# First loads of a fused QKV product: x by single row tiles between the k-tiles of the first weight block, each row tile cast and turned by itself

## The chip, the cores and the metric

The kernel runs on one core of a Trainium2 chip. A core has five engines with their own instruction streams: TensorE (PE in the profile, with its weight loads as PEld), VectorE (DVE), ScalarE (ACT), GpSimd (POOL) and SyncE (SP), which here only issues transfers. Sixteen DMA engines move data between HBM and the on-chip memory SBUF; PE writes its results into PSUM.

The metric is the device time of one execution in microseconds, lower is better. Runs of one kernel mostly agree within 0.2%. A change below 2% is classed as the same.

## The reference

```python
def setup_inputs():
    batch, seq, hidden = 16, 512, 768
    x = np.random.randn(batch, seq, hidden).astype(np.float32)
    w_qkv = np.random.randn(hidden, 3 * hidden).astype(np.float32)

def reference(x, w_qkv):
    qkv = np.matmul(x, w_qkv)          # 8192 x 768 times 768 x 2304
    q, k, v = ...                      # three column blocks of 768
    return np.stack([q, k, v], axis=0).astype(np.float32)
```

## The kernel before

x has 64 row tiles of 128 rows, handled in 32 pairs. w has four blocks of 512 columns and a remainder of 256 columns, each cut along the contraction into six k-tiles (KT = 6) of 128 rows. The first three pairs go through a plain bf16 product; from the fourth pair on, a form with seven products in place of eight is used, and by then all of w is on the chip. Only the start matters here.

Row tiles of x arrive in fp32 as rows and must be cast to bf16 and turned (transposed by PE through PSUM) before PE can use them; the k-tiles of w must be cast. While nothing has arrived, PE multiplies zeros (`busy`), to have its clock released.

```python
def load_rows(p):                      # a pair: two row tiles, one transfer of 786 kB
    xin[p] = xin_pool.tile([P, 2, K], fp32, name="xin")
    rows = x_flat[p * 2 * P:(p + 1) * 2 * P, :]
    nc.sync.dma_start(xin[p][:], rows.rearrange("(r m) k -> m r k", m=P))

def copy_halves(dst, src, two):        # half on DVE, half on ACT
    nc.vector.tensor_copy(out=dst[0], in_=src[0])
    if two:
        nc.scalar.activation(dst[1], src[1], ident)
    else:
        nc.vector.tensor_copy(out=dst[1], in_=src[1])

def turn_rows(p, two=True):            # cast_rows(p) is alike: fp32 -> bf16, by halves
    ...
    for r in range(2):
        cols = c[:, r, :].rearrange("m (p j) -> m j p", j=KT)
        ps = ps_pool.tile([P, KT, P], bf16, name="ps")
        for j in range(KT):
            nc.tensor.transpose(ps[:, j, :], cols[:, j, :], eye)
        ks = (slice(0, KH), slice(KH, KT))
        copy_halves([xb[p][:, n, r * P:(r + 1) * P] for n in ks], [ps[:, n, :] for n in ks], two)

# ---- order of the loads, all issued by SyncE
load_rows(0)
...
load_rows(1)
load_blocks(0, 0, 1)                   # six k-tiles of the first block, 262 kB each: k0..k5
load_w(st_rem[:], 0, KT, R_OFF, REM)   # the remainder, 786 kB
load_rows(2)
load_blocks(0, 1)                      # the next block in halves, and so on
...
# ---- order of the work
busy(11)
cast_rows(0)
turn_rows(0)
busy(4)
cast_rows(1)
cast_k(0)
cast_k(1)
turn_rows(1)
for j in range(2, KT):
    cast_k(j)
...                                    # remainder cast: half on ACT, half on DVE
block(0, 0, b1[0], singles, nothing)   # the first block, four row tiles, k-tile by k-tile
rem(0)
rem(1)
cast_rows(2, False)
turn_rows(2, False)
block(0, 0, b1[0], halves((4, 5)), nothing)
```

Of the kernel before, what the change touches and what calls it, by code (L numbers as in the profile page):

```python
# [10 lines left out]
def kernel(  # L11
# [20 lines left out]
    nc = tc.nc  # L32
    P = 128
# [3 lines left out]
    K = H  # L37
    N3 = w_qkv.shape[1]
    KT = K // P
    KH = KT // 2  # L40
    KC = K // 4
    NP = M // (2 * P)
    CB = 512
    REM = N3 - 4 * CB
    Q_OFF = (0, 2 * CB + REM)
    R_OFF = 2 * CB
    fp32 = mybir.dt.float32
    f32r = mybir.dt.float32r
    bf16 = mybir.dt.bfloat16
    ident = mybir.ActivationFunctionType.Identity  # L50
# [3 lines left out]
    x_flat = x.rearrange("b t h -> (b t) h")  # L54
# [5 lines left out]
    tq_pool = ctx.enter_context(tc.tile_pool(name="tq", bufs=2))  # L60
# [4 lines left out]
    xin_pool = ctx.enter_context(tc.tile_pool(name="xin", bufs=3))  # L65
    xf_pool = ctx.enter_context(tc.tile_pool(name="xf", bufs=2))
    xb_pool = ctx.enter_context(tc.tile_pool(name="xb", bufs=4))
    s_pool = ctx.enter_context(tc.tile_pool(name="s", bufs=2))
    ps_pool = ctx.enter_context(tc.tile_pool(name="ps", bufs=8, space=bass.MemoryType.PSUM))

    w_rem = w_pool.tile([P, KT, REM], bf16, name="w_rem")

    b1 = [w_pool.tile([P, KT, CB], bf16, name=f"b1_{q}") for q in range(2)]
# [7 lines left out]
    def load_w(dst, j0, nj, off, cols):  # L81
        rows = w_qkv.rearrange("(p j) n -> p j n", j=KT)
        nc.sync.dma_start(dst, rows[:, j0:j0 + nj, off:off + cols])

    stage = {}

    def load_blocks(q, c, nj=KH):
        if q == 0:
            t = tq_pool.tile([P, KT, CB], fp32, name="st0", tag="tq")
            for j in range(0, KT, nj):  # L90
                load_w(t[:, j:j + nj], j, nj, Q_OFF[q] + c * CB, CB)
            stage[q, 0, c], stage[q, 1, c] = t[:, :KH, :], t[:, KH:, :]
        else:
            for h in range(2):
                t = st_pool.tile([P, KH, CB], fp32, name="st1", tag="st")
                load_w(t[:], h * KH, KH, Q_OFF[q] + c * CB, CB)
                stage[q, h, c] = t[:]
# [11 lines left out]
    xin, xf, xb, sr = {}, {}, {}, {}  # L109
# [19 lines left out]



    def load_rows(p):
        xin[p] = xin_pool.tile([P, 2, K], fp32, name="xin")
        rows = x_flat[p * 2 * P:(p + 1) * 2 * P, :]
        nc.sync.dma_start(xin[p][:], rows.rearrange("(r m) k -> m r k", m=P))

    def copy_halves(dst, src, two):

# [5 lines that stand above are left out]

    xc = {}

    def cast_rows(p, two=True):
        src = xin.pop(p)
        xc[p] = s_pool.tile([P, 2, K], bf16, name="xc", tag="s")
        for r in range(2):  # L150
            halves = (slice(0, K // 2), slice(K // 2, K))
            copy_halves([xc[p][:, r, n] for n in halves], [src[:, r, n] for n in halves], two)

    def turn_rows(p, two=True):
        c = xc.pop(p)
        xb[p] = xb_pool.tile([P, KT, 2 * P], bf16, name="xb")
        for r in range(2):
            cols = c[:, r, :].rearrange("m (p j) -> m j p", j=KT)
            ps = ps_pool.tile([P, KT, P], bf16, name="ps")
            for j in range(KT):  # L160
                nc.tensor.transpose(ps[:, j, :], cols[:, j, :], eye)  # L161
            ks = (slice(0, KH), slice(KH, KT))
            copy_halves(
                [xb[p][:, n, r * P:(r + 1) * P] for n in ks], [ps[:, n, :] for n in ks], two
            )

    def round_x(p):
        xb[p] = xb_pool.tile([P, KT, 2 * P], bf16, name="xb")
# [42 lines left out]
    def bank():  # L211
        return ps_pool.tile([P, CB], fp32, name="ps")
# [29 lines left out]
    def rows_of(s, p, lo, hi):  # L242
        return out_flat[s, p * 2 * P:(p + 1) * 2 * P, lo:hi].rearrange("(r m) n -> m r n", m=P)

    def store_quad(u):
        if u.q == 0:
            nc.sync.dma_start(rows_of(0, u.p, 0, H), u.o[:, :, :H])
            nc.sync.dma_start(rows_of(1, u.p, 0, 2 * CB - H), u.o[:, :, H:])
        else:
            part = 2 * H - Q_OFF[1]  # L250
            nc.sync.dma_start(rows_of(1, u.p, H - part, H), u.o[:, :, :part])
            nc.sync.dma_start(rows_of(2, u.p, 0, H), u.o[:, :, part:])

    def rem_row(p, r, ps):
        for j in range(KT):
            nc.tensor.matmul(  # L256
                ps, xb[p][:, j, r * P:(r + 1) * P], w_rem[:, j, :],
                start=(j == 0), stop=(j == KT - 1), skip_group_check=True,
            )

    def rem(p):
        ps = ps_pool.tile([P, 2, REM], fp32, name="ps")
        for r in range(2):
            rem_row(p, r, ps[:, r, :])
        o = or_pool.tile([P, 2, REM], fp32, name="orem")
        nc.scalar.activation(o[:], ps[:], ident)  # L266
        nc.sync.dma_start(rows_of(1, p, R_OFF - H, R_OFF - H + REM), o[:])
# [70 lines left out]
    NS = 3  # L338
    zero = w_pool.tile([P, CB], bf16, name="zero")
    nc.vector.memset(zero[:], 0.0)  # L340
    load_rows(0)
    tiny = w_pool.tile([P, 1], fp32, name="tiny")
    nc.scalar.activation(tiny[:], zero[:, :1], ident)

    eye = w_pool.tile([P, 240], bf16, name="eye")[:, :P]
    make_identity(nc, eye)
    load_rows(1)
    load_blocks(0, 0, 1)
    st_rem = o_pool.tile([P, KT, REM], fp32, name="str", tag="o")
    load_w(st_rem[:], 0, KT, R_OFF, REM)  # L350
    load_rows(2)
    load_blocks(0, 1)
    load_blocks(1, 0)
    load_blocks(1, 1)
    load_x(3, nc.sync)
# [2 lines left out]
    def busy(n):  # L358

        ps = bank()  # L360
        for _ in range(n):
            nc.tensor.matmul(ps[:], zero[:, :P], zero[:], start=True, stop=True)  # L362
# [9 lines left out]
    def block(q, c, w, groups, cast_next):  # L372


        ps = {}
        for js, tiles in groups:
            for n in tiles:
                p, r = divmod(n, 2)
                if n not in ps:
                    ps[n] = bank()  # L380
                for j in js:
                    nc.tensor.matmul(  # L382
                        ps[n][:], xb[p][:, j, r * P:(r + 1) * P], w[:, j, :],
                        start=(j == 0), stop=(j == KT - 1), skip_group_check=True,
                    )
                if KT - 1 not in js:
                    continue
                if r == 0:
                    cast_next(p)
                u = quads[q][p]  # L390
                nc.scalar.activation(u.o[:, r, c * CB:(c + 1) * CB], ps[n][:], ident)
                if c == 1 and r == 1:
                    store_quad(u)

    def halves(tiles):
        return [(range(h * KH, (h + 1) * KH), tiles) for h in range(2)]


    singles = [((0, ), (0, 1)), ((1, ), (0, 1)), ((0, 1), (2, 3))]
    singles += [((j, ), range(4)) for j in range(2, KT)]  # L400

    act, dve = nc.scalar, nc.vector
    def cast_k(j):
        dve.tensor_copy(out=b1[0][:, j, :], in_=stage[0, j // KH, 0][:, j % KH, :])

    def cast_next(q, c, w):
        return lambda p: p < 2 and cast(q, p, c, w, act)

# [1 line left out]
        dve.tensor_copy(out=b1[0][:, j, :], in_=stage[0, j // KH, 0][:, j % KH, :])  # L410

    nothing = lambda p: None
    busy(11)
    cast_rows(0)
    turn_rows(0)
    busy(4)
    cast_rows(1)
    cast_k(0)
    cast_k(1)
    turn_rows(1)  # L420
    for j in range(2, KT):
        cast_k(j)
    act.activation(w_rem[:, KH:], st_rem[:, KH:], ident)
    dve.tensor_copy(out=w_rem[:, :KH], in_=st_rem[:, :KH])
    bt0 = bt_pool.tile([P, KT, CB], bf16, name="bt")
    bt1 = bt_pool.tile([P, KT, CB], bf16, name="bt")

    block(0, 0, b1[0], singles, nothing)
    rem(0)
    rem(1)  # L430
    cast_rows(2, False)
    turn_rows(2, False)
    block(0, 0, b1[0], halves((4, 5)), nothing)
    for h in range(2):
        cast(0, h, 1, bt0, dve)
    for n in range(1, 5):
        sum_w(0, n)
    dve.tensor_copy(out=b22[0][:], in_=stage[0, 1, 1])
    block(0, 1, bt0, halves(range(6)), cast_next(1, 0, b1[1]))
    load_x(4, nc.sync)  # L440
    block(1, 0, b1[1], halves(range(6)), cast_next(1, 1, bt1))
# [56 lines left out]
```

## Time and profile before

| | |
|---|---|
| time, median of 3 runs (later of 6) | 363.31 us (363.34) |
| span of the profiled execution | 362.0 us, itself a run of 363.8 us |
| PE busy | 353.5 us, 98% of the span |
| first real block matmul | 9.25 us |
| first remainder matmul | 14.43 us |
| first matmul of the next block | 20.61 us |
| last k-tile of the first block (k5) landed | 11.04 us |

The last four are the milestones to watch: all work of PE behind 20.61 us follows without a hole of note, so the end stands or falls with them.

### The profile page before, as it was taken

How to read it: one execution, taken by the hardware profiler on the slowest of the kernel's cores; microseconds unless marked ns; L12 is line 12 of the kernel's file. 1: busy time of each engine (PE TensorE's matmuls, PEld its weight loads, DVE VectorE, ACT ScalarE, POOL GpSimd, SP SyncE). 2: the span in 40 equal slices, each digit the busy share in tenths (PEclk: the TensorE clock that was granted, in tenths of full speed). 3: DMA queues.
4: the chain of work that ended last, by engine and by line, in shares of the span. 5: the costliest groups of instructions: out<-in, count | busy, mean ns of one | idle time of the engine just before them, and what ended most of it. 6: DMA issues, size and time to landing. Idle time of an engine off the chain costs nothing.

```text
span 362.0 us, 5220 instructions
## 1 busy us (share of the span) xinstructions
PE 353.5 (98%) x1765; PEld 248.6 (69%) x1797; DVE 224.4 (62%) x239; ACT 182.5 (50%) x304; POOL 174.1 (48%) x180
## 2 busy tenths in 40 slices
PE   8999999999999999999999999999999999999995
PEld 3644577777777776777777777777777777777763
DVE  3489746865566765566675565676556676556642
ACT  4547554445454545454545544444545454545452
POOL 0000960756664445664445665444666444666410
PEclk9999999999999999999999999999999999999999
DMA  7999969999999989899899999899989998989766
GB/s 295 381 381 339 346 224 343 331 304 298 278 321 298 295 275 295 282 313 313 284 277 294 281 306 316 281 283 285 295 284 317 295 295 274 300 275 332 266 251 242
DMA packets 80617, 108.08 MB, mean 299 GB/s; under 512 B 4816, under 2 KB 60368, under 8 KB 80592
## 3 DMA queue, kind: packets, MB, share of 16 engines
q1 hardware_dynamic: 65184, 96.35, 82.5%
q10 hardware_dynamic: 15408, 11.41, 9.7%
q8 instruction: 14, 0.23, 0.3%
q14 instruction: 11, 0.09, 0.1%
HBM read 32.24 MB, written 75.50 MB: 298 GB/s over the span
## 4 chain that ended last, share of the span: by engine, by line
PE 96%; ACT 1%; issue 1%; ACTq 0%; DVE 0%
PE ps L206 75%; PE ps L256 11%; PE ps L382 9%; PE ps L362 1%; PE ps L161 1%; ACT o L237 0%; ACTq L297 0%; ACT xb L141 0%; ACT orem L311 0%; DVE xb L139 0%; ACT xc L141 0%; ACTq L313 0%; DVE zero L340 0%; ACTq L311 0%
## 5 line engine op out<-in xcount | busy, mean ns | idle before, releaser
L206 PE MATMUL ps<-t,s 128*128 128x512 f32 x696 | 171.4, 395 | 0.0
L206 PEld LDWEIGHTS ps<-t,s 128*128 128x128 f32 x696 | 128.5, 188 | 26.5
L169 POOL CAST xb<-xf 128x1536 bf16<-128x1536 f32 x29 | 43.9, 1514 | 168.5 <-DVE xf L124 159.1
L234 DVE TENSOR_TENSOR o<-o,ps 128x512 f32<-128x512 f32 x58 | 39.9, 689 | 91.8 <-ACT o L233 91.8
L124 DVE STREAM_TRANSPOSE xf<-xin 128x1536 f32<-128x1536 f32 x29 | 85.5, 2950 | 5.7 <-DMA xin<-in_x_dram 2.9
L206 PE MATMUL ps<-b,xb 128*128 128x512 bf16 x320 | 74.2, 379 | 1.9
L206 PEld LDWEIGHTS <-xb 128*128 128x128 bf16 x348 | 31.7, 98 | 41.6 <-issue 7.3
L233 ACT ACTIVATE o<-ps 128x512 f32<-128x512 f32 x58 | 34.7, 598 | 44.7 <-PE ps L206 44.7
L240 DVE TENSOR_TENSOR o<-o,ps 128x512 f32<-128x512 f32 x58 | 39.9, 688 | 21.4 <-PE ps L206 20.2
L206 PE MATMUL ps<-b,s 128*128 128x512 f32 x174 | 48.7, 389 | 0.0
L256 PE MATMUL ps<-w_rem,xb 128*128 128x256 bf16 x384 | 47.2, 273 | 0.0
L266 ACT ACTIVATE orem<-ps 128x512 f32<-128x512 f32 x31 | 18.6, 601 | 56.3 <-PE ps L256 54.3
L237 ACT ACTIVATE o<-ps 128x512 f32<-128x512 f32 x58 | 34.7, 598 | 24.2 <-PE ps L206 21.4
L220 ACT ACTIVATE o<-ps 128x512 f32<-128x512 f32 x58 | 34.6, 597 | 23.8 <-DVE o L240 20.7
L256 PEld LDWEIGHTS <-xb 128*128 128x128 bf16 x384 | 37.4, 98 | 11.2 <-issue 0.5
L227 ACT ACTIVATE o<-ps 128x512 f32<-128x512 f32 x58 | 34.7, 599 | 6.6 <-PE ps L206 1.5
L224 DVE TENSOR_TENSOR o<-o,ps 128x512 f32<-128x512 f32 x58 | 36.4, 668 | 2.0 <-ACT o L220 1.3
L206 PEld LDWEIGHTS ps<-b,s 128*128 128x128 f32 x174 | 32.6, 188 | 6.9
L178 POOL TENSOR_TENSOR s<-s,xf 128x384 fp32r<-128x384 f32 x29 | 30.1, 1039 | 2.3
L177 POOL TENSOR_TENSOR s<-xf 128x384 fp32r<-128x384 f32 x29 | 31.0, 1069 | 0.0
L179 POOL TENSOR_TENSOR s<-xf 128x384 fp32r<-128x384 f32 x29 | 29.5, 1017 | 0.0
L181 POOL TENSOR_TENSOR s<-xf,s 128x384 fp32r<-128x384 f32 x29 | 29.5, 1016 | 0.0
(36 smaller groups left out, 129.3 us busy)
## 6 DMA issues: line engine op xcount, KB each, us to landing
out_dram<-o SPq DMA_DIRECT2D x62, 768.0 KB, 5.3
out_dram<-o SPq DMA_DIRECT2D x65, 256.0 KB, 4.5
xin<-in_x_dram SPq DMA_DIRECT2D x62, 192.0 KB, 6.7
xin<-in_x_dram ACTq DMA_DIRECT2D x54, 192.0 KB, 4.5
out_dram<-orem SPq DMA_DIRECT2D x31, 256.0 KB, 5.1
st<-in_w_qkv_dram SPq DMA_DIRECT2D x6, 768.0 KB, 14.1
xin<-in_x_dram SPq DMA_DIRECT2D x3, 768.0 KB, 5.7
st<-in_w_qkv_dram SPq DMA_DIRECT2D x6, 256.0 KB, 6.2
```

The source lines that it names most:

```text
L124: nc.vector.transpose(t[:].rearrange("p j (g b) -> p g j b", b=G), xin.pop(p)[:].rearrange("p g (a j) -> p g j a", a=G),)
L169: nc.gpsimd.tensor_copy(out=xb[p][:], in_=xf[p][:])
L206: nc.tensor.matmul(ps[:], lhs[j], rhs[j], start=(start and j == 0), stop=(j == KH - 1), skip_group_check=True,)
L220: nc.scalar.activation(c11, u.x[:], ident)
L224: nc.vector.tensor_tensor(c11, c11, u.z[:], op=add)
L227: nc.scalar.activation(c12, u.x[:], ident)
L233: nc.scalar.activation(c22, u.x[:], ident)
L234: nc.vector.tensor_tensor(c22, c22, u.y[:], op=add)
L237: nc.scalar.activation(c21, u.x[:], ident)
L240: nc.vector.tensor_tensor(c12, c12, u.y[:], op=add)
L256: nc.tensor.matmul(ps, xb[p][:, j, r * P:(r + 1) * P], w_rem[:, j, :], start=(j == 0), stop=(j == KT - 1), skip_group_check=True,)
L382: nc.tensor.matmul(ps[n][:], xb[p][:, j, r * P:(r + 1) * P], w[:, j, :], start=(j == 0), stop=(j == KT - 1), skip_group_check=True,)
```

## The change

The intent: give PE real work earlier. The first pairs of x come in row tiles of 393 kB, interleaved with the k-tiles, and every row tile is cast and turned as soon as it is there; PE then begins with two rows on two k-tiles while the rest is under way. The remainder and the third pair are cut in the same manner.

```diff
-    load_rows(0)
+    load_row(0, 0)                    # one row tile, [128, 768] fp32, 393 kB
 ...
-    load_rows(1)
-    load_blocks(0, 0, 1)
+    load_row(0, 1)
+    load_k(0)
+    load_k(1)
+    load_row(1, 0)
+    load_k(2)
+    load_row(1, 1)
+    for j in range(3, KT):
+        load_k(j)
-    load_w(st_rem[:], 0, KT, R_OFF, REM)
-    load_rows(2)
+    for h in range(2):
+        load_w(st_rem[:, h * KH:(h + 1) * KH], h * KH, KH, R_OFF, REM)
+    for r in range(2):
+        load_row(2, r)
 ...
-    busy(11)
-    cast_rows(0)
-    turn_rows(0)
-    busy(4)
-    cast_rows(1)
+    busy(8)
+    cast_row(0, 0)
+    cast_row(0, 1)
+    turn_row(0, 0)
+    busy(1)
     cast_k(0)
+    turn_row(0, 1)
     cast_k(1)
-    turn_rows(1)
 ...
+    def third_row():                  # busy(2), cast_row(1, 0), cast_k(2), turn_row(1, 0)
+    def fourth_row():                 # cast_row(1, 1), cast_k(3), turn_row(1, 1), cast_k(4), cast_k(5),
+                                      # then the remainder's cast, both halves on DVE
-    block(0, 0, b1[0], singles, nothing)
-    rem(0)
-    rem(1)
-    cast_rows(2, False)
-    turn_rows(2, False)
-    block(0, 0, b1[0], halves((4, 5)), nothing)
+    block(0, 0, b1[0], [
+        ((0, ), (0, 1)), ((1, ), (0, 1)), third_row,
+        ((2, ), (0, 1)), (range(3), (2, )), fourth_row,
+        ((3, ), range(3)), (range(4), (3, )), ((4, ), range(4)), ((5, ), range(4)),
+    ], nothing)
+    for p in range(2):
+        rem(p)
+        cast_row(2, p, False)
+        turn_row(2, p, False)
+    block(0, 0, b1[0], [(range(KT), (4, )), (range(KT), (5, ))], nothing)
```

More of the change, by code (lines that the diff above doesn't have):

```diff
@@ L128, in transpose, with load_row @@
         xf[p] = t
-    def load_rows(p):
-        xin[p] = xin_pool.tile([P, 2, K], fp32, name="xin")
-        rows = x_flat[p * 2 * P:(p + 1) * 2 * P, :]
-        nc.sync.dma_start(xin[p][:], rows.rearrange("(r m) k -> m r k", m=P))
+    def load_row(p, r):
+        if r == 0:
+            xin[p] = xin_pool.tile([P, 2, K], fp32, name="xin")
+        row = (2 * p + r) * P
+        nc.sync.dma_start(xin[p][:, r, :], x_flat[row:row + P, :])
     def copy_halves(dst, src, two):
@@ L145, with cast_row, turn_row @@
     xc = {}
-    def cast_rows(p, two=True):
-        src = xin.pop(p)
-        xc[p] = s_pool.tile([P, 2, K], bf16, name="xc", tag="s")
-        for r in range(2):
-            halves = (slice(0, K // 2), slice(K // 2, K))
-            copy_halves([xc[p][:, r, n] for n in halves], [src[:, r, n] for n in halves], two)
-    def turn_rows(p, two=True):
-        c = xc.pop(p)
-        xb[p] = xb_pool.tile([P, KT, 2 * P], bf16, name="xb")
-        for r in range(2):
-            cols = c[:, r, :].rearrange("m (p j) -> m j p", j=KT)
-            ps = ps_pool.tile([P, KT, P], bf16, name="ps")
-            for j in range(KT):
-                nc.tensor.transpose(ps[:, j, :], cols[:, j, :], eye)
-            ks = (slice(0, KH), slice(KH, KT))
-            copy_halves(
-                [xb[p][:, n, r * P:(r + 1) * P] for n in ks], [ps[:, n, :] for n in ks], two
-            )
+    def cast_row(p, r, two=True):
+        if r == 0:
+            xc[p] = s_pool.tile([P, 2, K], bf16, name="xc", tag="s")
+        halves = (slice(0, K // 2), slice(K // 2, K))
+        copy_halves([xc[p][:, r, n] for n in halves], [xin[p][:, r, n] for n in halves], two)
+    def turn_row(p, r, two=True):
+        if r == 0:
+            xb[p] = xb_pool.tile([P, KT, 2 * P], bf16, name="xb")
+        cols = xc[p][:, r, :].rearrange("m (p j) -> m j p", j=KT)
+        ps = ps_pool.tile([P, KT, P], bf16, name="ps")
+        for j in range(KT):
+            nc.tensor.transpose(ps[:, j, :], cols[:, j, :], eye)
+        ks = (slice(0, KH), slice(KH, KT))
+        copy_halves(
+            [xb[p][:, n, r * P:(r + 1) * P] for n in ks], [ps[:, n, :] for n in ks], two
+        )
     def round_x(p):
@@ L346, with load_k @@
     make_identity(nc, eye)
-    load_rows(1)
-    load_blocks(0, 0, 1)
-    st_rem = o_pool.tile([P, KT, REM], fp32, name="str", tag="o")
-    load_w(st_rem[:], 0, KT, R_OFF, REM)
-    load_rows(2)
-    load_blocks(0, 1)
+    st_0 = tq_pool.tile([P, KT, CB], fp32, name="st0", tag="tq")
+    stage[0, 0, 0], stage[0, 1, 0] = st_0[:, :KH, :], st_0[:, KH:, :]
+    def load_k(j):
+        load_w(st_0[:, j:j + 1], j, 1, Q_OFF[0], CB)
+    load_row(0, 1)
[6 more added lines that the diff above has]
+        load_k(j)
+    st_rem = o_pool.tile([P, KT, REM], fp32, name="str", tag="o")
+    for h in range(2):
+        load_w(st_rem[:, h * KH:(h + 1) * KH], h * KH, KH, R_OFF, REM)
+    for r in range(2):
+        load_row(2, r)
+    load_blocks(0, 1, KH)
     load_blocks(1, 0)
@@ L375, in block @@
         ps = {}
-        for js, tiles in groups:
+        for group in groups:
+            if callable(group):
+                group()
+                continue
+            js, tiles = group
             for n in tiles:
@@ L396, in halves @@
         return [(range(h * KH, (h + 1) * KH), tiles) for h in range(2)]
-    singles = [((0, ), (0, 1)), ((1, ), (0, 1)), ((0, 1), (2, 3))]
-    singles += [((j, ), range(4)) for j in range(2, KT)]
     act, dve = nc.scalar, nc.vector
-    def cast_k(j):
-        dve.tensor_copy(out=b1[0][:, j, :], in_=stage[0, j // KH, 0][:, j % KH, :])
     def cast_next(q, c, w):
@@ L412 @@
     nothing = lambda p: None
-    busy(11)
-    cast_rows(0)
-    turn_rows(0)
-    busy(4)
-    cast_rows(1)
+    busy(8)
[3 more added lines that the diff above has]
+    busy(1)
     cast_k(0)
+    turn_row(0, 1)
     cast_k(1)
-    turn_rows(1)
-    for j in range(2, KT):
-        cast_k(j)
-    act.activation(w_rem[:, KH:], st_rem[:, KH:], ident)
-    dve.tensor_copy(out=w_rem[:, :KH], in_=st_rem[:, :KH])
+    def third_row():
+        busy(2)
+        cast_row(1, 0)
+        cast_k(2)
+        turn_row(1, 0)
+    def fourth_row():
+        cast_row(1, 1)
+        cast_k(3)
+        turn_row(1, 1)
+        cast_k(4)
+        cast_k(5)
+        for h in range(2):
+            ks = slice(h * KH, (h + 1) * KH)
+            dve.tensor_copy(out=w_rem[:, ks], in_=st_rem[:, ks])
     bt0 = bt_pool.tile([P, KT, CB], bf16, name="bt")
     bt1 = bt_pool.tile([P, KT, CB], bf16, name="bt")
-    block(0, 0, b1[0], singles, nothing)
-    rem(0)
-    rem(1)
-    cast_rows(2, False)
-    turn_rows(2, False)
-    block(0, 0, b1[0], halves((4, 5)), nothing)
+    block(0, 0, b1[0], [
[8 more added lines that the diff above has]
+    block(0, 0, b1[0], [(range(KT), (4, )), (range(KT), (5, ))], nothing)
     for h in range(2):
```

## The prediction

> **What bounds the kernel now.** I read the page first (busy shares, then the chain that ended last), then the chain in order of time for the first 60 us, then the timelines of PE, DVE and ACT over the first 40 us, because the change touches nothing after them. From the page:
>
> ```profile
> PE 353.5 (98%) x1765; PEld 248.6 (69%) x1797; DVE 224.4 (62%) x239; ACT 182.5 (50%) x304; POOL 174.1 (48%) x180
> PE 96%; ACT 1%; issue 1%; ACTq 0%; DVE 0%
> ```
>
> PE is busy 98% of a span of 362.0 us and carries 96% of the chain. Whatever starts the real matmuls earlier moves the end by as much, as long as PE does not have to wait again later; nothing else can pay. So the prize is what PE does before it has real work. The chain in order of time (start us, us, what):
>
> ```profile
> 1.19 4.87 PE ps L362 x11
> 6.06 0.65 PE ps L161 x6
> ...
> 8.00 0.42 ACT xc L141
> 8.42 0.05 issue
> 8.47 0.95 PE ps L161 x12
> 9.42 2.16 PE ps L382 x10
> 11.57 0.05 issue
> 11.63 2.97 PE ps L382 x13
> 14.60 2.62 PE ps L256 x24
> 17.22 0.35 PE ps L161 x6
> 17.57 0.02 issue
> 17.59 0.37 DVE xb L139
> 17.96 0.05 issue
> 18.00 0.39 PE ps L382
> ```
>
> L362 is a matmul on zeros that keeps PE busy, L161 the transposes of x by PE, L382 the block matmuls, L256 the remainder columns. PE starts on real blocks at 9.25 us and then never rests for long: the one later hole is the turn of the third pair (17.57 to 18.00, 0.43 us). Before 9.25, real work is 24 transposes of 0.08 to 0.1 us, some 2.1 us; about 7 us of the first 9.25 are dummies or waiting. 7 us is 1.9% of 363.3, so even a perfect start would not reach 2%.
>
> What holds the start? The timeline of DVE (start us, us, instruction, the idle time before it and what ended it):
>
> ```profile
> 5.02 0.63 DVE L139 CAST xc<-xin 128x384 bf16<-128x384 f32 x2 [3.89 <-DMA xin<-in_x_dram]
> ...
> 11.06 0.43 DVE L410 CAST b<-st 128x512 bf16<-128x512 f32 x1 [0.24 <-DMA st<-in_w_qkv_dram]
> 13.30 0.56 DVE L424 CAST w_rem<-str 128x768 bf16<-128x768 f32 x1 [1.81 <-DMA str<-in_w_qkv_dram]
> 15.39 0.36 DVE L139 CAST xc<-xin 128x384 bf16<-128x384 f32 x1 [1.53 <-DMA xin<-in_x_dram]
> ...
> 20.95 0.96 DVE L370 CAST bt<-st 128x1536 bf16<-128x1536 f32 x1 [1.34 <-DMA st<-in_w_qkv_dram]
> ```
>
> DVE finds an empty input five times: the loads run at the pace of the DMA engines, and PE, with its work at 9.25, follows them closely. The trace's record of each landing gives: first pair of x rows 5.00 us, second 6.96, the six k-tiles of w 7.65, 8.31, 9.00, 9.68, 10.35, 11.04, the remainder columns 13.28, the third pair 15.27, the halves of the next block 17.30 and 20.92. A k-tile of 262 kB takes 0.68 us (385 GB/s), a pair of 786 kB 1.96 us (401 GB/s).
>
> **What the Trainium skill says.** "DMA: Bandwidth & Descriptors", Specifications, gives a fabric ceiling of 435 GB/s and an HBM limit of about 358 per core. The trace has 385 to 416 GB/s here, above the second and below the first; the measurement decides: the queue is already full, and smaller transfers will not make bytes arrive faster, only in another order. "TensorE: Matmul & The Clock Gate", Part 1, says that a matmul of 512 columns takes 426.7 ns on the idle clock and 215.7 on the full one, and that about 3.4 us of activity in a free-running window releases it. The trace agrees: the dummies are 0.43 us apart up to 5 us, 49 block matmuls take 10.74 us (219 ns each), and the clock record turns full at 6.64 us. Part 4 of that page says that transposes do not count as busy in the same way; no run shows this yet, and I use it as a risk.
>
> **The change part by part.** 4 of 15 dummies go (8, 1 and 2 remain). Each pair of rows comes in two transfers of 393 kB, between the k-tiles; the remainder in two as well. Row tiles are cast, turned and used singly, and PE's order is mixed: rows 0 and 1 on k-tiles 0 and 1, then row 2's turn, and so on. The remainder's cast goes from ACT and DVE to DVE alone in two halves. The third pair's turns are put one after each remainder product. Matmuls, transposes and bytes stay as they are. 4 transfers are added, which at 0.43 to 0.65 us of issue each stay ahead of 0.68 to 0.98 us of movement. The trace shows every ninth transfer being issued only when the first of the last eight landed (the ninth at 5.02, after 5.00; the tenth at 6.98, after 6.96); with smaller pieces, eight in flight are still above 2 MB, so the queue does not run dry.
>
> Landings, as estimates from those rates: row 0 at 4.0, row 1 at 5.0, k0 5.67, k1 6.34, row 2 7.3, k2 8.0, row 3 9.0, k3 9.66, k4 10.34, k5 11.0, remainder halves 12.15 and 13.28, rows 4 and 5 at 14.3 and 15.27. The last byte of each stage comes no sooner than before: k5 is where it was.
>
> PE then, with DVE casts and evictions of 0.35 to 0.37 us, ACT's of 0.49 to 0.52 (ACT's half of an eviction begins only where DVE's half ended: 7.13 after 6.74+0.37), k-tile casts of 0.42: 8 dummies end at 1.19+8x0.427=4.6, row 0 is turned by 5.3 and row 1 by 6.3. k0's cast ends at 6.2, row 1's eviction at 6.8, k1's cast at 7.2, so the first four block matmuls run from 6.3 to 7.7 with holes. Two dummies and row 2's turn take PE to 8.5, five matmuls to 9.6. Row 3 lands at 9.0, but ACT evicts row 2 first (9.0 to 9.47), so its cast ends at 9.99 and PE idles 0.4 us. Turn to 10.45, then 15 matmuls of 0.216 us = 3.24: 13.7 us against 14.43 before. The remainder's halves are cast by 12.7 and 13.84, in time to within 0.1.
>
> From there: 12 remainder matmuls 1.31, row 4's turn 0.42, 12 more 1.31 (16.75), row 5's turn after its cast (16.75 to 17.2), 12 block matmuls 2.59: the next block begins at 19.8 against 20.61. **Sum: 0.8 us**: 0.7 from the block that ends earlier (14.43-13.7), and 0.1 from the stretch after it, 6.18 us before (14.43 to 20.61, with its hole) and 6.1 now. All the rest of PE's work moves up by that, if the later inputs are there: the second half of the next block is cast by 21.9 and needed at 19.8+18x0.216=23.7; the block after lands at 22.79 and 24.82, needed at 27.5 and 31.4. In the first strided pair, PE needs the sums for its third product at about 48 and POOL has them by 43.0. In the later stage POOL is ahead by over 2 us. So the shift should reach the end whole.
>
> **Rivals.** (1) The clock is released later. PE is active from 1.19 in both, but in 3.1 to 6.5 us the new kernel has more transposes and only some 2 us of dummies. If the transposes don't count, the full clock comes 3.4 us later; about nine matmuls and two dummies at double time cost 2.3 us of which the waits for k-tiles absorb much, and the block ends near 14.4: gain 0.1 to 0.2. For: the skill; against: PE has hardly a gap there. One in four. (2) The loads bound all of it: k5, the remainder and row 5 land where they were, and the change yields nothing. Against: in the kernel before, PE begins the remainder 3.4 us after k5 lands, so there is something to win there. But the remainder's second half, landed at 13.28 and cast by 13.84, lets the second group of its matmuls go no earlier than that, which caps the gain near 0.9, and row 5 at 15.27 caps it near 1.5. (3) The extra turns between DVE and ACT cost more than is won: each of four row turns is a round of cast, transposes and two evictions in series, 0.35+0.65+0.37+0.49 us. If each waited 0.3 us more than I reckon, the block would end at 14.6 and the change would be neutral or 0.3 us slower. (4) Gain lost later: DMA engines are busy over 90% in the whole span, so loads of later x pairs might not move up and PE would give it back. The slack of over 2 us speaks against.
>
> **Range and chances.** Central step sum 363.3-0.8=362.5; weighting the later clock and the slower hand-overs, I take 362.6. The three runs before differ by 0.22 us; gains from -0.1 to 1.3 us give 362.0 to 363.4. 2% is 7.3 us, more than all the idle time at the start, so faster by that is out of reach; slower by that would need a stall of a kind that nothing here shows.
>
> **What would show it right or wrong.** First row cast at 4.0 us; first block matmul near 6.3; k5's cast at about 11.4 to 11.8; first remainder matmul at 13.7; first matmul of the next block at 19.8; the same landings from the remainder on. Full clock at 6.6 us in both kernels; if the dummies or matmuls near 8 us are 0.43 us apart, rival 1 holds. If the first remainder matmul waits for its cast, rival 2; if PE's waits at the row turns sum to over 1.5 us between 6.3 and 13.7, rival 3; if 19.8 is met but the end is not moved, rival 4. I am wrong in kind if the time moves by over 1.5 us either way.

## The result, and the profile after

The changed kernel took 363.81 us (median of 6 runs, 363.52 to 364.00) against 363.34 us for the kernel before in the same rounds (363.23 to 363.90). The ratio is 1.001 with a 95% interval of 0.9997 to 1.0023. A ratio is computed as the mean time of one kernel's runs over that of the other's of the same rounds, so it is not quite the ratio of the medians. The change is worth nothing, and leans to the slow side; I had predicted 362.6 us with 362.0 to 363.4 as the range.

The page of the changed kernel, the lines of busy time and of the chain by engine:

```profile
PE 352.8 (98%) x1761; PEld 247.4 (68%) x1793; DVE 225.6 (62%) x240; ACT 182.2 (50%) x303; POOL 173.8 (48%) x180
PE 95%; DMA 1%; ACT 1%; issue 1%; ACTq 0%; SPq 0%; DVE 0%
```

A new entry stands in the chain, DMA with 1%. The chain in order of time (start us, us, what) shows where it is:

```profile
2.12 4.96 DMA st<-in_w_qkv_dram
7.08 0.02 issue
7.10 0.44 DVE b L422
...
7.58 0.59 PE ps L401 x2
...
14.33 1.40 PE ps L255 x12
15.72 0.53 PE ps L160 x6
16.25 1.31 PE ps L255 x12
17.56 0.48 PE ps L160 x6
```

Before, the chain ran through PE's dummies and turns from 1.19 us on. Now it runs through one transfer of w, issued at 2.12 us and landed at 7.08: k1. The timeline of DVE shows the same from the side of the one who waits:

```profile
3.71 0.36 DVE L140 CAST xc<-xin 128x384 bf16<-128x384 f32 x1 [2.58 <-DMA xin<-in_x_dram]
...
5.62 0.43 DVE L422 CAST b<-st 128x512 bf16<-128x512 f32 x1 [0.15 <-DMA st<-in_w_qkv_dram]
...
7.10 0.43 DVE L422 CAST b<-st 128x512 bf16<-128x512 f32 x1 [0.75 <-DMA st<-in_w_qkv_dram]
...
13.95 0.56 DVE L448 CAST w_rem<-str 128x768 bf16<-128x768 f32 x1 [0.56 <-DMA str<-in_w_qkv_dram]
15.03 0.36 DVE L140 CAST xc<-xin 128x384 bf16<-128x384 f32 x1 [0.52 <-DMA xin<-in_x_dram]
```

k0 is cast at 5.62, as early as I had reckoned. k1 comes 1.48 us after it, where a k-tile took 0.68 us before. That transfer is the only one on the chain: from the end of k1's cast at 7.53 to the next block the chain is work alone, and the second trace of this kernel (e0_after) has the same shape, with k1 landing at 7.44. Everything behind is late by about that difference: k5 landed at 11.70 us instead of 11.04, the remainder's second half is cast from 13.95 instead of 13.30, the first remainder matmul starts at 14.16 instead of the 13.7 that I expected, and the next block at 20.47 instead of 19.8.

The rate of the loads over the first 10 us, in 40 slices of a quarter of a microsecond, first of the kernel before, then of the changed one:

```profile
GB/s 0 0 0 0 0 0 0 147 74 61 283 319 418 393 430 418 418 406 430 418 418 406 418 414 402 389 418 402 402 401 385 393 377 393 393 385 385 385 385 381
DMA packets 1340, 3.04 MB, mean 304 GB/s; under 512 B 113, under 2 KB 114, under 8 KB 1340
```

```profile
GB/s 0 0 0 0 0 0 0 233 184 246 307 418 381 356 418 381 340 340 344 271 205 184 254 254 369 369 414 389 332 389 279 381 397 414 422 356 385 393 385 418
DMA packets 1243, 2.80 MB, mean 280 GB/s; under 512 B 131, under 2 KB 131, under 8 KB 1243
```

Before, the rate stays at or above 377 GB/s from 3 us on. After, it falls to between 184 and 344 from 4 to 6 us. In ten microseconds 0.24 MB less arrive. The trace's record of single packets tells part of how: a packet of 2 kB normally takes 84 ns and one of 3 kB 121 ns. Between 3 and 8 us the changed kernel has 20 packets above 250 ns, the longest 1028 ns; the kernel before has none, its longest being 124 ns. I call them slow packets below. The count leaves out what comes before 3 us, where every kernel has some: 3 to 16 of them begin between 2 and 3 us, 7 in the kernel before and 9 in the changed one.

The count marks a disturbed start, but does not measure the loss. An estimate from these records: the 20 packets took 9.0 us together, where 15 of 2 kB and 5 of 3 kB would take 1.9 at their usual times; over 16 engines the difference is 0.44 us, of the 0.66 by which k5 was late. In the second trace of the changed kernel it is 0.34 of 1.0 us, in e6 below 0.15 of 0.9. From 3 to 7 us the time of all packets also fell from 102.8% to 95.2% of the sixteen engines' time, so engines stood without a packet more often than before.

### The profile page after: what moved, and what is told of

Its sections match the earlier page's. It is cut to its first block, busy times and chain, and to the rows that moved or that the text cites. A ratio compares the mean times of both kernels' runs of the same rounds, so it can differ in the third digit from the quotient of the medians.

```text
span 361.7 us, 5215 instructions
## 1 busy us (share of the span) xinstructions
PE 352.8 (98%) x1761; PEld 247.4 (68%) x1793; DVE 225.6 (62%) x240; ACT 182.2 (50%) x303; POOL 173.8 (48%) x180
## 4 chain that ended last, share of the span: by engine, by line
PE 95%; DMA 1%; ACT 1%; issue 1%; ACTq 0%; SPq 0%; DVE 0%
PE ps L205 75%; PE ps L255 11%; PE ps L401 8%; DMA st<-in_w_qkv_dram 1%; PE ps L160 1%; ACT o L236 0%; ACTq L296 0%; SPq L136 0%; ACT orem L310 0%; ACT xb L142 0%; DVE b L422 0%; PE ps L376 0%; SPq L83 0%; ACT xc L142 0%; ACTq L312 0%
```

## The experiments

My theory after the result is D: the interleaved order of the first loads makes them slower, and all of the lost gain is in that. Its rivals are E, that not the order but the cut into smaller transfers does it; H, that the new hand-overs between DVE, ACT and PE cost more than I reckoned; and C, that the moment of the clock's release is behind it. First all measurements in one table (e2 and t5 each had one run, of 367.1 and 366.7, that stands apart; the medians are hardly moved by it): times as medians against the kernel before of the same rounds, and from the trace of each run the landing of k5, the count of packets above 250 ns between 3 and 8 us, the start of the first block matmul and of the next block's, all in us.

| run | time | before | ratio (95%) | k5 landed | slow packets | first block | next block |
|---|---|---|---|---|---|---|---|
| before (first trace) | 363.34 | | | 11.04 | 0 | 9.25 | 20.61 |
| after (first trace) | 363.81 | 363.34 | 1.0010 (0.9997-1.0023) | 11.70 | 20 | 6.10 | 20.47 |
| e0_before | 363.59 | 363.28 | 1.0005 (0.9993-1.0017) | 10.99 | 0 | 9.21 | 20.56 |
| e0_after | 363.73 | 363.28 | 1.0009 (0.9997-1.0021) | 12.03 | 21 | 7.16 | 20.81 |
| e1_rows_first | 367.41 | 363.28 | 1.0109 (1.0096-1.0122) | 12.62 | 23 | 9.72 | 24.00 |
| e2_old_compute_new_loads | 364.90 | 363.28 | 1.0053 (1.0033-1.0072) | 11.67 | 23 | 10.55 | 21.91 |
| e3_pairs_between | 364.38 | 363.36 | 1.0027 (1.0014-1.0039) | 11.69 | 19 | 7.34 | 21.34 |
| e4_first_pair_whole | 364.50 | 363.36 | 1.0030 (1.0018-1.0043) | 11.70 | 18 | 7.30 | 21.58 |
| e5_cut_only | 364.56 | 363.36 | 1.0027 (1.0013-1.0041) | 12.51 | 22 | 9.65 | 21.53 |
| e6_cut_by_columns | 364.05 | 363.36 | 1.0021 (1.0008-1.0033) | 11.95 | 6 | 9.21 | 21.01 |
| g1_third_pair_only | 363.38 | 363.29 | 0.9997 (0.9985-1.0009) | 11.01 | 2 | 9.27 | 20.48 |
| v1_split_banks | 362.97 | 363.29 | 0.9988 (0.9975-1.0001) | 11.02 | 1 | 8.35 | 19.84 |
| t5_order_only | 364.91 | 363.29 | 1.0050 (1.0034-1.0065) | 11.48 | 15 | 10.19 | 21.54 |
| u1_new_compute_old_loads | 365.53 | 363.29 | 1.0058 (1.0046-1.0070) | 11.03 | 0 | 8.14 | 22.53 |
| p1_third_pair_first | 365.32 | 363.27 | 1.0055 (1.0040-1.0070) | 12.99 | 2 | 8.21 | 22.43 |
| p2_two_queues | 363.99 | 363.27 | 1.0017 (1.0000-1.0034) | 11.52 | 8 | 7.72 | 20.98 |
| p3_before_look | 363.19 | | one run | 10.97 | 0 | 8.68 | 20.05 |
| p4_before_look | 363.27 | | one run | 11.02 | 0 | 8.72 | 20.10 |

Each run has one trace, and the runs lie on four chips. With two whole pairs first, k5 landed at 10.97 to 11.03 on each of three of them. The fourth (e3 to e6) has no such trace, but two of its orders were also run elsewhere and agree: e5's first ten transfers are those of e1 (k5 at 12.51 and 12.62), e3's are those of t5 (11.69 and 11.48).

### Both kernels again

No edit.

> The kernel before, unchanged, for a second trace and for the noise of a ratio of a kernel to itself. All theories: ratio 1.000 within 0.001. Theory C (the moment at which the TensorE clock is released varies from run to run) expects a release elsewhere than at 6.64 us and, where it is earlier, a span of about 361.5 us; theories D (the interleaved order of loads costs 0.7 us of transfer time) and H (the row by row hand-overs cost it) expect the tenth transfer (k5) to land at 11.0 again.

> The changed kernel, unchanged, for a second trace. Ratio to before 1.0010 to 1.0015 in all theories. D expects that single packets of the first transfers again take several hundred ns and that k5 lands near 11.7 instead of 11.0; if k5 lands at 11.0 to 11.1 and the time is still 0.5 us longer than before, D is wrong and H or C is left.

A kernel against itself gave 1.0005, so half of a thousandth is noise. The second trace of the changed kernel repeats the picture: 21 slow packets, k5 even later at 12.03, and the next block at 20.81. On its chain the entry of k1 reads:

```profile
2.11 5.33 DMA st<-in_w_qkv_dram
```

Between the two traces of the changed kernel k1 moved by 0.36 us, k5 by 0.33 and the next block by 0.34: PE follows the loads nearly one for one.

### Order and cut of the loads, one at a time

The changed kernel with its cut, but with the old order (rows first):

```diff
     load_row(0, 1)
+    load_row(1, 0)
+    load_row(1, 1)
-    load_k(0)
-    load_k(1)
-    load_row(1, 0)
-    load_k(2)
-    load_row(1, 1)
-    for j in range(3, KT):
+    for j in range(KT):
         load_k(j)
```

> The changed kernel with its cut into single rows and its PE order, but with the four rows loaded before the six k-tiles, as before. D: k5 lands at 11.0 again, 0.7 us sooner than in the changed kernel, and no packet takes above 0.3 us after 3 us; but the PE order wants k0 and k1 before row 2, so PE is held by k1 at 8.3 and the block ends near 14.7: time 363.8 to 364.3. H: k5's landing as in the changed kernel (11.7), or the cut itself at fault.

This missed, and D with it: k5 came at 12.62, the latest of all but p1 (which loads a pair more ahead of it), with a packet of 1553 ns among rows 2 and 3. The order cannot be the only culprit; the cut alone, in the old order, does more harm. The time of 367.4 also holds a loss of another kind, told further down with the clock.

The kernel before with the ten first transfers as in the changed one, and its own work otherwise:

```diff
-    load_rows(0)          # ... load_rows(1); load_blocks(0, 0, 1)
+    load_row(0, 0)        # row, row, k0, k1, row, k2, row, k3, k4, k5
```

> The kernel before with only its first ten transfers cut and ordered as in the changed kernel; casts, turns and PE order as before. D: k5 lands at 11.6 to 11.8, as in the changed kernel, though no engine's work has changed. H: k5 at 11.0 to 11.1. In both, the second pair is complete only with row 3 (9.0 to 9.7), so its turn comes late and the time is 1 to 1.6 us above before.

k5 at 11.67, with the work of every engine unchanged. H is out as the cause of the late landings.

The changed kernel with the first two pairs whole, in the new places:

```diff
-    load_row(0, 0); load_row(0, 1); load_k(0); load_k(1); load_row(1, 0); load_k(2); load_row(1, 1)
+    load_rows(0); load_k(0); load_k(1); load_rows(1); load_k(2)
```

> The changed kernel with the first two pairs of x loaded whole again ([2,128] rows of 3 kB in one transfer), in the new places between the k-tiles; rows still cast and turned singly. E (the cut into single-row transfers makes single packets of the first transfers take up to 1.5 us; the order does not): first pair lands at 5.0, k1 6.3, second pair 8.3, k5 at 11.0 as before, no packet over 0.3 us after 3 us, and the time 362.4 to 363.0, faster than both kernels by 0.3 to 0.9 us. D (the interleaved order costs it): k5 at 11.5 to 11.8 and time 363.5 or more. H (hand-overs): k5 at 11.0 and yet 363.5 or more.

And with only the first pair whole:

```diff
-    load_row(0, 0)
+    load_rows(0)
 ...
-    load_row(0, 1)
```

> The changed kernel with only its first transfer made whole (rows 0 and 1 in one), rows 2 and 3 cut. E, if what counts is that the transfers behind the first are issued far ahead of their data: k5 at 11.0 to 11.2, time 362.5 to 363.1. E, if each cut row costs: k5 at 11.2 to 11.6. D: k5 at 11.5 to 11.8.

Both landed k5 at 11.7. E alone was too narrow as well: without any cut of x, in e3, the second pair behind k1 met the same slow packets. I had hoped that e3 would beat both kernels; it was 1.0 us slower than before. Not all of that is the loads: in the traces of e3 and e4 the full clock came only at 9.52 and 10.04 us, and their first block matmuls ran at half of it.

The kernel before with nothing but the cut into rows, and with a cut of the same size by columns:

```diff
# e5                                    # e6
-    load_rows(0)                       -    load_rows(0)
+    for r in range(2):                 +    for h in range(2):
+        load_row(0, r)                 +        load_cols(0, h)     # [128, 2, 384]
-    load_rows(1)                       -    load_rows(1)
+    for r in range(2):                 +    for h in range(2):
+        load_row(1, r)                 +        load_cols(1, h)
```

> The kernel before with its first two pairs loaded as four single rows, nothing else changed, order of loads as before. E: packets of 0.4 to 1.5 us between 4 and 6 us, k5 at 12.0 to 12.8 (before 11.0), and 0.8 to 1.8 us slower than before. D: k5 at 11.0, time as before.

> The kernel before with each of its first two pairs loaded as two column halves (again [2,128] pieces, of 1.5 kB): as many transfers of as many bytes as the cut into rows, but two pieces to a partition. If the form of one piece to a partition is at fault: k5 at 11.0 to 11.3 and time within 0.3 us of before. If the number or the size of the first transfers is at fault: k5 at 12.0 or later, 0.8 us slower or more.

The cut alone brings slow packets and delays k5 by 1.5 us in e5 and by 0.9 in e6. Single row tiles are worse than column halves of the same number of bytes, but a cut of either form brings a loss; neither expectation for e6 fits cleanly.

The kernel before with nothing but another order, no transfer cut:

```diff
-    load_rows(1)
-    load_blocks(0, 0, 1)
+    # k0, k1, then
+    load_rows(1)
+    # k2 .. k5
```

> The kernel before with k0 and k1 loaded before the second pair, no transfer cut, nothing else changed. If the order alone brings the slow packets: packets of 0.4 us and more between 5 and 6.6 us, k5 at 11.6 to 11.8, and the second pair, wanted first by PE, at 8.9: 1.5 to 2 us slower than before. If only the cut does: k5 at 11.0, second pair at 8.3, 1.0 to 1.4 us slower.

The order alone brings 15 slow packets and delays k5 by 0.45 us. The rates of the cut alone and of the order alone, in the same slices as above:

```profile
GB/s 0 0 0 0 0 0 37 209 172 160 406 430 344 258 344 356 320 357 381 369 320 184 184 295 303 340 393 426 361 352 381 369 348 393 393 418 393 401 418 410
```

```profile
GB/s 0 0 0 0 0 0 0 172 86 37 246 246 455 418 406 418 389 401 414 402 410 406 389 442 209 233 356 393 406 381 373 385 401 385 344 418 377 385 410 393
```

Both dip to about 200 GB/s between 5 and 6.5 us, and the cut has an earlier dip at 3.25 too.

### The other half of the cross: new work, old loads

```diff
-    load_row(0, 0); load_row(0, 1); load_k(0); load_k(1); load_row(1, 0); ...
+    load_rows(0); load_rows(1); load_k(0); ... load_k(5)
```

> The changed kernel with the first eight transfers as before: both pairs whole, then the k-tiles. The loads should be as before (k5 at 11.0, no long packets after 3 us). PE's new order wants k0 and k1 first, so its first block matmul comes at 8.1 and, with PE idle before, the clock may be released late: 0.5 to 1.5 us slower than before. If k5 lands at 11.6 or later here too, it is not the order and cut of the loads that slow them but something in the new compute.

```profile
GB/s 0 0 0 0 0 0 0 184 49 61 233 344 406 393 418 418 455 418 393 418 406 406 406 418 418 393 410 410 410 393 393 385 377 393 393 393 385 377 393 377
```

With the old first transfers the new work leaves the loads alone: no slow packet, k5 at 11.03, the rate of the kernel before. With e2 this closes the cross. The slow packets past 3 us come with the order and the cut of the first transfers, and not with the work of the engines, new or old.

The time, however, went to 365.5, at the end of what I expected. Busy time by windows shows why (columns: window, PE, PEld, DVE, ACT, POOL busy, granted PE clock, DMA share, GB/s):

```profile
4.63:8.04 3.41, 1.23 (x14) 0.99 (x14) 1.36 (x5) 1.43 (x3) 0.00 (x0) 1.00 1.03 404
8.04:11.45 3.41, 3.31 (x13) 1.66 (x13) 1.41 (x5) 0.90 (x2) 0.00 (x0) 0.50 1.07 376
```

PE waited for x and then for k0 and was busy for only 1.23 of 3.41 us; the next 3.41 us were granted at half the clock, in which its matmuls take twice as long. The same befell e1 (half clock again from 9.87 to 13.28 us, after 3.42 us in which PE was busy for 0.19), which is part of why its time is so bad, and p1 below. In these three traces an order of work that left PE waiting cost it the clock as well; no run here filled those waits with zeros.

### Where the slow packets belong

The changed kernel with the third pair loaded whole, ahead of everything:

```diff
+    nc.sync.dma_start(xin[2][:], ...)          # 786 kB, whole pair
     load_row(0, 0)
 ...
-    for r in range(2):
-        load_row(2, r)
```

> The changed kernel with the third pair of x (786 kB, whole) loaded ahead of everything, so that its interleaved single rows and k-tiles move 2 us later, from 4.3 us on; the same bytes in all. If the slow packets belong to the first 6.5 us of the run (start-up): none after 6.6 us, few in all, the last k-tile at 13.0 to 13.3. If they belong to the interleaved order and the cut as such, they come again 2 us later and the last k-tile lands at 13.6 to 14.0. Time 1 to 3 us above before in both, since PE starts 2 us later.

```profile
GB/s 0 0 0 0 0 0 0 147 74 74 246 344 406 393 406 418 455 418 418 393 393 393 381 406 418 397 410 393 418 422 406 414 393 410 381 401 410 418 393 393
```

The very same interleaved rows and k-tiles, now moved from 4.3 us on, run at full rate. k5 landed at 12.99 us, which is 11.03 plus the 1.96 us of the pair ahead of it, to the hundredth. So interleaving and cutting did no harm here, and are not slow wherever they stand. What protects them p1 does not settle, for it changes two things: they move later, and a whole pair is ahead of them. The pair alone is not enough: e4 begins with a whole pair too, and has 18 slow packets between 4.7 and 6.5 us. Nor is it the time alone: from 4.3 to 6.2 us p1 moves two single rows without a dip, where e5 dips.

The changed kernel with k0, k1 and k2 issued by ACT on its own queue:

```diff
+    for j in range(3):
+        load_k(j, nc.scalar)                   # before ACT's first instruction
 ...
     load_row(0, 1); load_row(1, 0); load_row(1, 1)
+    for j in range(3, KT):
+        load_k(j, nc.sync)
```

> The changed kernel with k0, k1, k2 issued by ACT on its own queue at the start, so that they share the DMA engines with the rows that SyncE issues. If slow packets come from the order in one queue: none here, k5 at 11.0 to 11.2, time 362.6 to 363.3. If they come with any mixture of short transfers in the first 6.5 us: k5 at 11.6 to 12.2, time 363.5 to 364.5.

Neither expectation fits. There were eight packets of 273 to 519 ns between 2.7 and 3.2 us (six of them past 3 us, so in the table's count) and only two later; k5 landed at 11.52. The loss fell into the ramp of the first microseconds, 303 GB/s or less until 3.5 us, instead of the dip at 5 us. The time, 363.99, is no better than that of the changed kernel.

### The baseline: why the kernel before has two times

> The kernel before, one more look. Its times fall into two groups, 363.2 to 363.3 and 363.6 to 363.9, and both traces so far are of the second, with the full clock from 6.5 to 6.6 us. If this run is of the first group, theory C expects the full clock before 6 us and the first block matmul before 9.0 us; k5 at 11.0 in any case.

> As the run above, once more, to catch a run of the other group. k5 at 11.0 and no packet over 0.3 us between 3 and 7 us.

Both looks caught the faster group, at 363.19 and 363.27 us. In these traces the granted clock turns full at 5.38 and 3.85 us, in the two slower ones (363.80 and 363.69) at 6.64 and 6.48. In the chain of the slower e0_before, then of p3 (start us, us, what):

```profile
6.06 0.61 PE ps L161 x6
...
8.42 0.95 PE ps L161 x12
9.37 2.16 PE ps L382 x10
```

```profile
1.19 4.60 PE ps L362 x11
5.79 0.35 PE ps L161 x6
...
7.89 0.95 PE ps L161 x12
8.84 2.16 PE ps L382 x10
```

With the clock released before the first turn, the six transposes on the chain take 0.35 us in place of 0.61 and start 0.27 earlier, and the first block begins 0.53 us sooner. Theory C holds for this: the release varies by up to 2.8 us between executions of one and the same kernel, and is worth 0.5 us. Past that it is worth no more: p4, released 1.5 us before p3, was no faster, and both releases came before the first turn. It does not explain the result of the change: the traces of the changed kernel had their release at 4.44 and 5.38 us, early, and were still at 20.47 and 20.81 where an early kernel before is at 20.05 to 20.10.

### The later part alone, and a version with the lowest median

The kernel before with only the remainder in halves (cast by DVE) and the third pair by rows, each turned after one remainder product:

```diff
-    rem(0)
-    rem(1)
-    cast_rows(2, False)
-    turn_rows(2, False)
+    for p in range(2):
+        rem(p)
+        cast_row(2, p, False)
+        turn_row(2, p, False)
```

> The kernel before with only the later part of the change: the remainder loaded and cast in two halves on DVE, the third pair loaded, cast and turned a row at a time, each row after one remainder product. The first eight transfers are untouched. All theories that put the loss into the first loads: k5 at 11.0, no long packet after 3 us, the hole of 0.43 us at the third pair's turn closed: 0.2 to 0.4 us faster than before, 362.9 to 363.2. H (the new hand-overs themselves cost): no gain or slower.

Less than expected: 363.38 against 363.29, no difference. Its trace had the late clock (6.71 us) and put the next block at 20.48, 0.1 us ahead of the late traces of before. The hole of 0.43 us is gone, but the second row's transposes had lain inside that hole; now they stand on the path. That is how 0.43 shrinks to 0.1. Cutting the transfers here, from 12 us on, left k5 at 11.01, and two packets above 250 ns between 3 and 8 us did no harm.

The same, and each turned row of the first two pairs in two PSUM tiles:

```diff
-            ps = ps_pool.tile([P, KT, P], bf16, name="ps")
+            pss = [ps_pool.tile([P, KH, P], bf16, name="ps") for _ in range(2)]
             for j in range(KT):
-                nc.tensor.transpose(ps[:, j, :], cols[:, j, :], eye)
+                nc.tensor.transpose(pss[j // KH][:, j % KH, :], cols[:, j, :], eye)
```

> The run above and, besides, each turned row of the first two pairs put into two PSUM tiles, so that ACT's half of an eviction need not wait for DVE's half. If that wait (0.4 us a row) is on the path to the first block matmul: first block matmul 0.3 to 0.5 us earlier than in the run above, 362.5 to 362.9. If something else (the casts on ACT) holds it: as the run above.

The timeline of ACT in the kernel before (p3) and in this one:

```profile
6.55 0.87 ACT L141 ACTIVATE xb<-ps 128x384 bf16<-128x384 bf16 x2 [0.65 <-DVE xb L139]
7.31 0.93 ACT L141 ACTIVATE xc<-xin 128x384 bf16<-128x384 f32 x2
```

```profile
6.14 0.91 ACT L147 ACTIVATE xb<-ps 128x384 bf16<-128x384 bf16 x2 [0.22 <-PE ps L167]
6.98 0.94 ACT L147 ACTIVATE xc<-xin 128x384 bf16<-128x384 f32 x2
```

ACT's half now waits for PE and no longer for DVE, and its casts of the second pair start as soon as the pair has landed (6.95). Compared with p3, whose clock was released at nearly the same time (5.38, here 5.34 us), the first block starts 0.33 us earlier and the next block 0.21. The median of 362.97 us is the best, below before (363.29, ratio 0.9988) and below the changed kernel (363.81); but the interval reaches 1.0001, so by the measure it is the same as before. Its five runs, 362.85 to 363.10, all lie below every run of before (363.20 to 364.04 in those rounds).

## Why the prediction was wrong

The class was right (within 2%, and "even a perfect start would not reach 2%"). The amount was not: I forecast 0.7 us less, and measured about 0.5 more (0.47 and 0.45 by the medians of two rounds; both intervals still include no change).

**The step that failed is the line of landings, "as estimates from those rates": k1 at 6.34 us, row 2 at 7.3, k5 at 11.0.** I took 385 and 401 GB/s from the kernel before and held that smaller transfers "will not make bytes arrive faster, only in another order", with "k5 is where it was". The two traces of the changed kernel showed k1 at 7.08 and 7.44, row 2 at 8.03 and 8.39, and k5 at 11.70 and 12.03. The rates were those of a queue that starts with two whole pairs. Each of the six distinct sequences that took the place of that start (after and e2; e1 and e5; e3 and t5; e4; e6; p2) lost 0.45 to 1.6 us by k5. I had checked whether the queue would run dry and found that it would not; this was right, and beside the point: when row 1 landed at 4.82 us six transfers were issued and outstanding, and yet the rate fell.

**The work between was reckoned well, with some luck.** I put the next block at 19.8 with k5 at 11.0, a distance of 8.8 us. Measured were 8.77 (20.47 - 11.70) and 8.78 (20.81 - 12.03). But k5 is not on the chain: it landed at 11.70, and by my count of matmuls PE needs it only at about 13.5 (an estimate, four matmuls of 0.216 us before 14.33). It moved along with what PE did wait for. Step by step, against my times: k1's cast ended at 7.53 instead of 7.2 (0.33 late; I had left k1 0.46 us of slack behind row 1's eviction), row 2's turn at 9.18 instead of 8.5 (0.68 late), row 3's turn at 11.09 instead of 10.45 (0.64), and the next block began 0.67 late. So half of the loss stands at k1. The rest is there by the end of row 2's turn, where two things fall together: row 2 landed 0.73 late, and its turn took 0.55 us where my times leave it 0.37. From there on the sum held to 0.04 us.

The first row cast came at 3.71 (I said 4.0), the first block matmul at 6.10 (6.3). Rival 3, dearer hand-overs, did not reach its mark: over the window from 6.1 to the first remainder matmul at 14.16 PE was busy for 7.09 of 8.06 us, so it waited for 1.0 us, under the 1.5 that I had named. (The prediction's own example for rival 3 is a slip: four turns 0.3 us later each end the block at 14.9, not at 14.6.)

**The baseline was mis-sized by 0.4 to 0.5 us.** I subtracted 0.8 us, found against a trace with the next block at 20.61, from a median of 363.3. But that trace was of a run of 363.8 with a late clock; a run of 363.2 to 363.3 has the next block at 20.05 to 20.10. My own 19.8, with the distance of 342.9 to 343.3 to the end in all eighteen traces, meant 362.7 to 363.1. The central sum was 362.5, and the two traced runs of the changed kernel took 363.52 and 363.91. Split at the next block, the misses of 1.0 and 1.4 us are 0.67 and 1.01 us of landing and work before it, and 0.35 and 0.4 us of baseline. This is a division of the miss and not a check of it, since the distance to the end is taken from the same runs.

**Rivals and marks.** Rival 1, a late clock, did not occur in the two traces of the changed kernel (4.44 and 5.38 us), but "full clock at 6.6 us in both kernels" was wrong as a statement: it ranges from 3.85 to 6.71 us where the first window of work suffices, and to 10.04 in e4. Rival 2, the loads, came closest to the truth, though not as I had put it: k5, the remainder and row 5 did not land where they were, but later. That part I had not thought of. Its mark did not show: the first remainder matmul came at 14.16, right behind the block and 0.8 us after the cast of its first half. Rival 4 is refuted by the constant distance to the end. Of the hole at the third pair I expected 0.1 us, and g1 bears it out, as far as 0.1 us can be told.

**What stays open.** The runs show in which starts packets past 3 us are slow (most of them before 6.5 us, though in the changed kernel 7 of the 20 began between 6.5 and 7.9; not where the first 1.6 MB come as two whole pairs, and not in p1, where a whole pair and two rows come first), and that it does not depend on the engines' work. They do not show why, nor what else beside the slow packets makes the landings late. The trace does not tell which of the sixteen DMA engines moved a packet, so whether single engines lag or all are stopped together is not settled; in e3 eleven packets that began between 5.80 and 6.03 us ended between 6.40 and 6.64, which looks like the second, while in the changed kernel single packets of about 1 us stand among normal ones.

## What to carry to other kernels

A transfer rate read from a trace belongs to the sequence of transfers in that trace: before a plan rests on landings in another order or size, above all in the first microseconds of a run, load them once on the chip and read the landings and the packets' durations. Before a gain is subtracted from a median, check that the traced run is one of the median's kind; here the trace was 0.5 us off, which is more than half of the gain forecast. And when two engines empty one PSUM tile by halves and the second waits for the first, try two tiles: in v1 that wait went away, and the first block began 0.33 us earlier.

## What the Trainium skill lacked or had wrong

- "DMA: Bandwidth & Descriptors" (Latency and other measured facts; Specifications) gives an HBM access latency of 0.2 us on average and 2 us at high load. The slow packets of 0.25 to 1.55 us lie between, but the page does not say that they gather at the start of a run and depend on how the first transfers are cut and ordered: between 3 and 8 us 15 to 23 of them with row tiles or k-tiles in between (6 with column halves, 8 with two queues), 0 to 2 with two whole pairs first. Its HBM limit of about 358 GB/s for a core is too low for this stage, with one core running: the kernel before moved 377 to 430 GB/s from 3 to 10 us.
- "TensorE: Matmul & The Clock Gate" (Part 1) says that the clock falls back after at least one idle window of about 3.4 us. In u1 it fell to half after a window of 3.41 us in which PE was busy for 1.23 us, and in p1 after 1.21 of 3.42 us: a window need not be idle. With 2.29 of 3.41 us (the changed kernel) it stayed full. The windows' length of 3.41 us and a release that varies agree with the page, but here it varies from 3.85 to 6.71 us where the page gives 0.5 us either way.
- "PSUM — Partial Sum Buffer" (PSUM bank collisions raise a hardware error) says that two engines must be kept off the same 32 partitions of one bank at a time, reads included. This agrees with ACT's waiting for DVE on one tile (0.65 us in p3) and with its going away with two tiles (v1).
